# A hybrid encoder step on one core: the durations by which vector steps are woven between matrix products

## The chip, the cores and the metric

The kernel runs on one core of a Trainium2 chip. The metric is the device time of one execution in microseconds, the median of the runs shown. Its engines are named as in the profile: PE does matrix products, DVE elementwise vector work, ACT activations, POOL nearly nothing here, and SP issues the transfers.

## The reference

Two layers act on 1024 prompt rows and 32 sample rows of width 1024, with shared weights. Layer 0 mixes with a gated MLP, layer 1 with trailing means over windows of 2, 4, 8 and 16 rows. Each mixer is followed by a feed-forward of width 4096. Norms stand on both sides of each, and a conditioning vector gives shifts, scales and gates. Cut to its core:

```python
for i in range(DEPTH):                       # DEPTH = 2
    mod = jax.nn.silu(c) @ w_ada[i] + b_ada[i]
    sh1, sc1, gt1, sh2, sc2, gt2 = jnp.split(mod[:, None, :], N_MOD, axis=-1)
    h = rmsnorm(x, g_norm[i, 0]) * (1 + sc1) + sh1
    mix = sgu_mixer(h, ...) if i % 2 == 0 else pool_mixer(h_ext, ...)
    x = x + gt1 * rmsnorm(mix, g_norm[i, 1])
    h = rmsnorm(x, g_norm[i, 2]) * (1 + sc2) + sh2
    f = jnp.square(jax.nn.relu(h @ ffn_w_up[i])) @ ffn_w_down[i]
    x = x + gt2 * rmsnorm(f, g_norm[i, 3])
```

All of it is float32; the outputs are the two sequences and three small states.

## The kernel before

Columns are rows of the sequence: activations lie transposed, features on the partitions. There are three column tiles `t`: 384 and 384 prompt columns, and a last one of 256 prompt and 32 sample columns, so its elementwise work goes in two segments (`segs`). Per tile there is `acc[t]`, the running sum and later the residual stream, and `hh[t]` and `hl[t]`, the high and low parts of the normed input. Every product is three matrix products (`products`, L720 to L725): high weight by high input, high by low, low by high. A weight block is loaded to `raw`, copied to the high part `wh` on ACT (L342) and subtracted to the low part `wl` on DVE (L343).

**Order of the products.** The gating mixer works in groups `g` (`sgu_item`), the feed-forward in chunks `c` of 512 hidden features (`ffn_item`). Each item has an up part (`pu`, or `pf` in four blocks) and a down part (`po` or `pg`, eight blocks `d`), which adds into `acc[t]` on DVE (L875). The down part is held in `pending` and is written out in the middle of the next item. For layer 0 the last groups and chunks (6, 7) are done tile by tile, and for layer 1 the first chunks (0, 1) too, so that one tile's mixer or feed-forward can end, be normed and feed the next stage while the other tiles still have products. A down block whose item has an `after` ends a tile: it also squares each `acc` block for the norm (`Stat.square`).

**Fillers.** What happens to a tile between two stages is a generator, kept in `fillers`: `ffn0_t` (from gating mixer to feed-forward 0), `ffn1_t` (from feed-forward 0 through pooling mixer to feed-forward 1) and `out_t`. Its pieces are `Stat.finish` (the norm: two small products `pn` over the split sums `sc` and `sm`, L610 to L632), `residual` (gate and add the old stream, which is loaded again from memory, L644 to L672), `apply` (scale on DVE L689, shift on ACT L698, low part on DVE L699), the window sums (L1191 to L1219) and the mixing products `pp` (L1240). A generator yields after each step a number, the step's duration in us as the program counts it; a negative one says that the same filler goes on next. `weave(budget, streams)` is called after each block of products: it first does up to `streams` steps of the weight stream (1.1 each for a weight), then pulls filler steps until the budget is spent. Every third pull takes the second filler instead of the first. `finish(tag)` pulls until the named filler is through; it is called before the first chunk of a feed-forward needs that tile:

```python
while budget > 0 and fillers:
    budget -= pull()
...
if c == 0:
    finish(f"ffn{l}_{t}")
ffn_item(p, t, after if c == 7 else None)
```

The numbers set only the order in which instructions are written. The tile framework then places them on the engines; each engine works through its own queue in order and waits on semaphores. Sums sit in PSUM buffers: three for down parts (`pd`, which `pp` and early products share), two for up parts (`pu`), three for norms and transposes (`pm`).

Of the kernel before, what the change touches and what calls it, by code (L numbers as in the profile page):

```python
# [34 lines left out]
def tile_stream_encoder_step(  # L35
# [32 lines left out]
    def pool(name, **kw):  # L68
# [8 lines left out]
    ncol = [p + s for _, p, s in TILES]  # L77
    segs = [
        [(0, p, 0)] + ([(p, s, 1)] if s else []) for _, p, s in TILES
    ]  # L80
# [70 lines left out]
    for i, parts in enumerate(rows):  # L151
        n = sum(k for _, k in parts)
# [363 lines left out]
        wdone.add(key)  # L516


    fillers = deque()

    sticky = []
# [54 lines left out]
    class Stat:  # L576
# [42 lines left out]

        def finish(self, out):  # L620
            n = self.n
            yield 0.5
            pn = ps_ms(f"pn_{self.tag}")
            for i, x in enumerate(self.parts):
                mm(pn[:, :n], onesr, x[:, :n], start=i == 0, stop=i == 1)
            yield 0.3
            q = t_m(f"q_{self.tag}")[:, :n]
            r = work.tile([P, 384], F32, tag="rr", bufs=2, name=f"r_{self.tag}")[:, :n]
            act(out=r, in_=pn[:, :n], func=AF.Abs_reciprocal_sqrt, scale=1.0 / D)
            act(out=q, in_=r, func=AF.Square)  # L630
            stt(out=q, in0=pn[:, :n], scalar=-0.5 / D, in1=q, op0=ALU.mult, op1=ALU.mult)
            stt(out=r, in0=q, scalar=1.5, in1=r, op0=ALU.add, op1=ALU.mult)  # L632
            out.append(r)
            yield 2.0


    def residual(st, l, cf, tag, out, store=True, stat=True):
        t = st.t
        n = ncol[t]
        xos = {}  # L640

        def load(k2):
            xos[k2] = t_x(f"xo_{tag}_{k2}", [P, 2, n])
            nc.sync.dma_start(xos[k2], xd[t][:, 2 * k2 : 2 * k2 + 2, :])  # L644

        got = []
        yield from st.finish(got)
        r = got[0]
        st2 = Stat(t, tag + "x")
        for half in range(2):  # L650
            for k2 in (2 * half, 2 * half + 1):
                load(k2)
            for k2 in (2 * half, 2 * half + 1):
                for k in (2 * k2, 2 * k2 + 1):
                    for c0, w, v in segs[t]:
                        a = A(t, k, c0, w)
                        stt(
                            out=a,
                            in0=a,
                            scalar=coef[:, l, cf, v, k : k + 1],  # L660
                            in1=r[:, c0 : c0 + w],
                            op0=ALU.mult,
                            op1=ALU.mult,
                        )
                    yield -0.46
                a = acc[t][:, 2 * k2 : 2 * k2 + 2, HALO:]
                tt(out=a, in0=a, in1=xos[k2], op=ALU.add)
                if stat:
                    st2.square(2 * k2, a)
                yield 0.9 if k2 % 2 else -0.9  # L670
        if store:
            nc.sync.dma_start(xd[t], acc[t][:, :, HALO:])  # L672
        out.append(st2)
# [8 lines left out]
    def apply(t, l, cf, sh, r, keep=False):  # L682
        hh[t] = room("h", t, f"hh{l}_{cf}_{t}", F32R)
        hl[t] = room("l", t, f"hl{l}_{cf}_{t}", F32R)
        for k in range(KB):
            for c0, w, v in segs[t]:
                x = A(t, k, c0, w)
                a = t_m(f"mt{t}_{k}_{v}")[:, :w] if keep else x
                stt(  # L689
                    out=a,  # L690
                    in0=x,
                    scalar=coef[:, l, cf, v, k : k + 1],
                    in1=r[:, c0 : c0 + w],
                    op0=ALU.mult,
                    op1=ALU.mult,
                )
                b = mod[:, l, sh * 8 + k, v : v + 1]
                act(out=hh[t][:, k, c0 : c0 + w], in_=a, func=AF.Identity, bias=b, scale=1.0)  # L698
                stt(  # L699
                    out=hl[t][:, k, c0 : c0 + w],  # L700
                    in0=a,
                    scalar=b,
                    in1=hh[t][:, k, c0 : c0 + w].bitcast(F32),
                    op0=ALU.add,
                    op1=ALU.subtract,
                )
            yield 0.95

    def first_norm(t):
        n = ncol[t]  # L710
# [189 lines left out]
    def sgu_item(g, t, wt, bb, after):  # L900
        n = ncol[t]
# [65 lines left out]
        def down():  # L967
            for d in range(KB):
                ps = ps_dn(f"po{g}_{t}_{d}")
                wh, wl = need_w(("o", g, d // 4))  # L970
                terms = []
                for k in range(2):
                    o = k * 512 + (d % 4) * P
                    a, b = hid[k]
                    terms.append((wh[:, o : o + P], wl[:, o : o + P], a[:, :n], b[:, :n]))
                products(ps, n, terms)
                accumulate(t, d, ps, g == 0)
                if d == 0 and after is not None:
                    st = Stat(t, f"rs_{t}")
                if after is not None:  # L980
                    st.square(d)
                if t == NT - 1 and d % 4 == 3:
                    w_finish(("o", g, d // 4))
                weave(0.4, d % 2)
            if after is not None:
                after(st)

# [7 lines left out]
    def ffn_item(p, t, after):  # L995
        l, c, tiles = passes[p]
        last = t == tiles[-1]
        n = ncol[t]
        hid = []

        def up(j):
            ps = ps_up(f"pf{l}_{c}_{t}_{j}")
            products(ps, n, up_terms(("up", p, j), t))
            if last:
                w_finish(("up", p, j))
            r = t_m(f"r{l}_{c}_{t}_{j}")
            act(out=r[:, :n], in_=ps[:, :n], func=AF.Relu)  # L1007
            a, b = t_hid("h", f"fh{l}_{c}_{t}_{j}"), t_hid("l", f"fl{l}_{c}_{t}_{j}")
            act(out=r[:, :n], in_=r[:, :n], func=AF.Square)
            split(a, b, r, n)  # L1010
            hid.append((a, b))

        def down():
            for d in range(KB):
                ps = ps_dn(f"pg{l}_{c}_{t}_{d}")
                wh, wl = need_w(("dn", p, d // 2))
                terms = []
                for j in range(4):
                    o = j * 256 + (d % 2) * P
                    a, b = hid[j]  # L1020
                    terms.append((wh[:, o : o + P], wl[:, o : o + P], a[:, :n], b[:, :n]))
                products(ps, n, terms)
                accumulate(t, d, ps, c == 0)
                if d == 0 and after is not None:
                    st = Stat(t, f"rf{l}_{t}", l == 0 or t < NT - 1)
                if after is not None:
                    st.square(d)
                    if l == 1 and t == NT - 1:
                        scale_last(d)
                        if d > 0:  # L1030
                            turn_last(d - 1)
                if last and d % 2 == 1:
                    w_finish(("dn", p, d // 2))
                weave(1.3, d % 2)
            if after is not None:
                after(st)

        for j in range(4):
            up(j)
            weave(3.0)  # L1040
            if j == 0:
                flush()
        pending.append(down)


# [62 lines left out]
    def to_pool(st):  # L1108
        t = st.t
        n = ncol[t]  # L1110
        npr, nsm = TILES[t][1], TILES[t][2]

        def run():
# [25 lines left out]
            for k in range(KB):  # L1139
                for c0, w, v in segs[t]:  # L1140
                    a = A(t, k, c0, w)
                    stt(
                        out=a,
                        in0=a,
                        scalar=coef[:, 1, 0, v, k : k + 1],
                        in1=r[:, c0 : c0 + w],
                        op0=ALU.mult,
                        op1=ALU.mult,
                    )
                    dst = a if v == 0 else pool_ext["e"][:, k, 16 : 16 + w]  # L1150
                    act(
                        out=dst,
                        in_=a,
                        func=AF.Identity,
                        bias=mod[:, 1, k, v : v + 1],
                        scale=1.0,
                    )
                yield 0.5
            if t == 0:
                nc.vector.memset(acc[0][:, :, 0:HALO], 0.0)  # L1160
            if t + 1 < NT:
# [21 lines left out]
            for src, w, dst0, nm in parts:  # L1183
                for g in range(4):
# [3 lines left out]
                    for lev in range(g + 1):  # L1188
# [7 lines left out]
                        )  # L1196
                        cur = nxt
                        step *= 2
                        yield -0.9
                    body = cur[:, :, HALO:]  # L1200
                    hsrc = src[:, 2 * g : 2 * g + 2, HALO:]
                    dst = acc[t][:, 2 * g : 2 * g + 2, HALO + dst0 : HALO + dst0 + w]
# [21 lines left out]
                        op0=ALU.mult,  # L1224
                        op1=ALU.subtract,
                    )
                    yield 1.0 if g == 3 else -1.0

            sp = Stat(t, f"rp_{t}")
            for g in range(4):  # L1230
# [11 lines left out]
                for e in range(2):  # L1242
                    d = 2 * g + e
                    act(out=A(t, d), in_=pss[e][:, :n], func=AF.Copy, scale=pscale[:, d : d + 1])
                    sp.square(d)
                yield 0.3
            yield from mix_to_ffn(sp, 1)

        fillers.append((f"ffn1_{t}", run()))
# [124 lines left out]
```

## Time and profile before

| | us |
|---|---|
| runs before, median (lowest to highest) | 2258.66 (2256.62 to 2258.75) |
| profiled execution | 2254.32 |
| its span, first to last instruction | 2252.5 |
| mean granted clock of PE | 0.994 |
| PE busy | 2205.2 |
| DVE busy | 1308.7 |
| ACT busy | 867.9 |

The span is one execution of the program under the hardware profiler, and 1.8 us of that execution's own time lie outside it. Busy time is the sum of an engine's instructions. Each row of a wait names who waited, for whom, and the total, count and longest wait in us. A window row gives, for a stretch of the span, its length, each engine's busy time and instructions, the granted PE clock as a share of full speed, the share of the DMA engines, and GB/s. Stages by time: conditioning and value products to 293 us, gating groups to about 680, feed-forward 0 to about 1470, feed-forward 1 to the end.

### The profile page before, as it was taken

The page shows a single profiled execution, that of the slowest core. Times are in us where ns is not written, and L with a number is a line of the kernel's source. Part 1 is how long each engine was busy: PE and PEld are TensorE (multiplying, and loading weights), DVE is VectorE, ACT ScalarE, POOL GpSimd, SP SyncE. Part 2 cuts the span into 40 slices and gives each one's busy share as a digit, 9 for nine tenths or more (in the row PEclk, how much of TensorE's full clock was granted, in tenths as well). Part 3 has the DMA queues.
Part 4 walks back from the last instruction along what each step waited for, and adds up shares of the span by engine and source line. Part 5 has one row for each costly group of instructions (what it writes and reads, how often), then busy time and mean ns, then how long its engine had stood idle before and what let it go on. Part 6 is the DMA issues. An engine that isn't in the chain of part 4 may idle for free.

```text
span 2252.5 us, 33484 instructions
## 1 busy us (share of the span) xinstructions
PE 2205.2 (98%) x13508; PEld 2099.6 (93%) x13508; DVE 1308.7 (58%) x2677; ACT 867.9 (39%) x1579; POOL 0.7 (0%) x6
## 2 busy tenths in 40 slices
PE   7999999999999999999999999899999999999998
PEld 5777899999989999999999999789899999999998
DVE  4855756555698366584654579999752322323345
ACT  4633521112256413223232466676652322313334
POOL 0000000000000000000000000000000000000000
PEclk9999999999999999999999999999999999999999
DMA  8465532122143223233332454664550211202112
GB/s 295 149 225 163 179 98 84 60 72 67 53 133 106 94 85 113 85 120 95 95 103 71 134 157 148 195 181 153 190 169 10 66 38 38 75 10 66 41 50 91
DMA packets 269631, 245.34 MB, mean 109 GB/s; under 512 B 8642, under 2 KB 247690, under 8 KB 269476
## 3 DMA queue, kind: packets, MB, share of 16 engines
q1 hardware_dynamic: 269204, 243.10, 34.5%
q8 instruction: 106, 1.74, 0.3%
q14 instruction: 49, 0.40, 0.1%
q10 hardware_dynamic: 272, 0.10, 0.0%
HBM read 211.32 MB, written 31.84 MB: 108 GB/s over the span
## 4 chain that ended last, share of the span: by engine, by line
PE 90%; DVE 4%; ACT 2%; DMA 2%; issue 1%; SPq 0%; DVEq 0%; ACTq 0%
PE pf L723 11%; PE pf L724 11%; PE pf L725 11%; PE pg L723 10%; PE pg L724 10%; PE pg L725 10%; PE pu L723 3%; PE po L723 3%; PE pu L724 3%; PE pu L725 3%; PE po L724 3%; PE po L725 3%; PE pv L748 2%; PE pv L749 2%; PE pv L750 2%; PE psp L929 1%
## 5 line engine op out<-in xcount | busy, mean ns | idle before, releaser
L723 PE MATMUL pf<-hh,wh_up 128*128 128x384 f32 (+1 forms) x1536 | 499.8, 326 | 4.3 <-ACT hh L698 3.7
L724 PE MATMUL pf<-hl,wh_up 128*128 128x384 f32 (+1 forms) x1536 | 498.8, 325 | 1.2 <-DVE hl L699 1.2
L723 PE MATMUL pg<-fh,wh_dn 128*128 128x384 f32 (+1 forms) x1536 | 497.8, 325 | 1.0 <-DVE acc L875 0.9
L725 PE MATMUL pf<-hh,wl_up 128*128 128x384 f32 (+1 forms) x1536 | 497.1, 324 | 0.0
L724 PE MATMUL pg<-fl,wh_dn 128*128 128x384 f32 (+1 forms) x1536 | 495.4, 323 | 1.1 <-DVE fl L868 1.1
L725 PE MATMUL pg<-fh,wl_dn 128*128 128x384 f32 (+1 forms) x1536 | 494.8, 322 | 0.0
L875 DVE TENSOR_TENSOR acc<-acc,pg 128x384 f32<-128x384 f32 (+1 forms) x336 | 173.7, 519 | 271.2 <-PE pg L725 270.2
L723 PEld LDWEIGHTS pf<-hh,wh_up 128*128 128x128 f32 x1536 | 289.1, 188 | 9.0 <-ACT hh L698 4.2
L723 PEld LDWEIGHTS pg<-fh,wh_dn 128*128 128x128 f32 x1536 | 289.0, 188 | 4.6 <-issue 2.0
L724 PEld LDWEIGHTS pg<-fl,wh_dn 128*128 128x128 f32 x1536 | 289.1, 188 | 2.8 <-DVE fl L868 2.1
L724 PEld LDWEIGHTS pf<-hl,wh_up 128*128 128x128 f32 x1536 | 289.4, 188 | 2.1 <-DVE hl L699 1.5
L725 PEld LDWEIGHTS pf<-hh,wl_up 128*128 128x128 f32 x1536 | 289.3, 188 | 0.4
L725 PEld LDWEIGHTS pg<-fh,wl_dn 128*128 128x128 f32 x1536 | 288.9, 188 | 0.0
L414 DVE SCALAR_TENSOR_TENSOR aa<-raw,csil,aa 128x256 f32<-128x256 f32 x560 | 233.0, 479 | 3.2 <-DMA raw<-in_w_ada_dram 3.2
L1007 ACT ACTIVATE r<-pf 128x384 f32<-128x384 f32 (+1 forms) x192 | 87.5, 458 | 372.0 <-PE pf L725 357.1
L868 DVE TENSOR_TENSOR fl<-r,fh 128x384 fp32r<-128x384 f32 (+1 forms) x192 | 100.3, 522 | 179.9 <-ACT fh L867 165.6
L342 ACT ACTIVATE wh_up<-raw 128x1024 fp32r<-128x1024 f32 x96 | 101.6, 1058 | 262.7 <-PE pf L724 244.5
L343 DVE TENSOR_TENSOR wl_up<-raw,wh_up 128x1024 fp32r<-128x1024 f32 x96 | 117.5, 1224 | 122.2 <-ACT wh_up L342 122.0
L342 ACT ACTIVATE wh_dn<-raw 128x1024 fp32r<-128x1024 f32 x96 | 101.6, 1059 | 120.8 <-PE pg L724 107.2
L343 DVE TENSOR_TENSOR wl_dn<-raw,wh_dn 128x1024 fp32r<-128x1024 f32 x96 | 117.4, 1223 | 46.7 <-ACT wh_dn L342 46.6
L723 PE MATMUL po<-ush,wh_o 128*128 128x384 f32 (+1 forms) x384 | 127.5, 333 | 3.4 <-DVE acc L875 3.1
L723 PE MATMUL pu<-hh,wh_u 128*128 128x384 f32 (+1 forms) x384 | 126.6, 330 | 1.6 <-DVE s L945 1.6
(260 smaller groups left out, 2978.2 us busy)
## 6 DMA issues: line engine op xcount, KB each, us to landing
raw<-in_w_ada_dram SPq DMA_DIRECT2D x96, 512.0 KB, 3.9
raw<-in_ffn_w_up_dram SPq DMA_DIRECT2D x96, 512.0 KB, 4.1
raw<-in_ffn_w_down_dram SPq DMA_DIRECT2D x96, 512.0 KB, 3.4
raw<-in_sgu_w_in_dram SPq DMA_DIRECT2D x32, 512.0 KB, 4.6
xd<-acc SPq DMA_DIRECT2D x8, 1536.0 KB, 7.3
xo_r<-xd SPq DMA_DIRECT2D x32, 384.0 KB, 3.8
vd<-vt SPq DMA_DIRECT2D x32, 256.0 KB, 2.7
raw<-in_sgu_w_out_dram SPq DMA_DIRECT2D x16, 512.0 KB, 3.5
```

The lines of the kernel that those rows point to most:

```text
L342: act(out=wh, in_=r, func=AF.Copy)
L343: tt(out=wl, in0=r, in1=wh.bitcast(F32), op=ALU.subtract)
L414: stt(out=aa[:, v, :], in0=w, scalar=k, in1=aa[:, v, :], op0=ALU.mult, op1=ALU.add)
L723: mm(ps[:, :n], wh, rh, start=i == 0, stop=False)
L724: mm(ps[:, :n], wh, rl, start=False, stop=False)
L725: mm(ps[:, :n], wl, rh, start=False, stop=i == last)
L748: mm(ps[:m, :], a_h, wh[:, o : o + 512], start=k == 0, stop=False)
L749: mm(ps[:m, :], a_h, wl[:, o : o + 512], start=False, stop=False)
L750: mm(ps[:m, :], a_l, wh[:, o : o + 512], start=False, stop=k == KB - 1)
L868: tt(out=dst_lo[:, :n], in0=src[:, :n], in1=dst_hi[:, :n].bitcast(F32), op=ALU.subtract)
L875: tt(out=A(t, d), in0=A(t, d), in1=ps[:, :n], op=ALU.add)
L1007: act(out=r[:, :n], in_=ps[:, :n], func=AF.Relu)
```

## The change

A helper `dve(n, parts)` counts 0.15 us for each instruction and one 960th of a microsecond for each column. The fixed step numbers of norm, residual, modulation, windows and mixing are replaced by it. The residual's second step also counts the squares that it issues. In blocks that end a tile, the weave budget of the gating mixer's down block goes from 0.4 to 0.0, and that of the feed-forward's down block from 1.3 to 0.8.

For 384 columns `dve(n)` is 0.55, for two blocks of 384 columns 0.95, for 288 columns 0.45 and in two segments 0.60.

```diff
+    def dve(n, parts=1):
+        return 0.15 * parts + n / 960.0
...
         def finish(self, out):
             n = self.n
-            yield 0.5
+            yield dve(n)
             pn = ps_ms(f"pn_{self.tag}")
...
             out.append(r)
-            yield 2.0
+            yield 2 * dve(n)
...
     def residual(st, l, cf, tag, out, store=True, stat=True):
...
-                    yield -0.46
+                    yield -dve(n, len(segs[t]))
                 a = acc[t][:, 2 * k2 : 2 * k2 + 2, HALO:]
                 tt(out=a, in0=a, in1=xos[k2], op=ALU.add)
+                cost = dve(2 * n)
                 if stat:
                     st2.square(2 * k2, a)
-                yield 0.9 if k2 % 2 else -0.9
+                    cost += (k2 > 0) * dve(2 * n) + (k2 == 3) * 2 * dve(n)
+                yield cost if k2 % 2 else -cost
...
     def apply(t, l, cf, sh, r, keep=False):
...
-            yield 0.95
+            yield 2 * dve(ncol[t], len(segs[t]))
...
# sgu_item, down
-                weave(0.4, d % 2)
+                weave(0.4 if after is None else 0.0, d % 2)
...
# ffn_item, down
-                weave(1.3, d % 2)
+                weave(1.3 if after is None else 0.8, d % 2)
...
# to_pool: modulation, window levels, window ends, mixing
-                yield 0.5
+                yield dve(n, len(segs[t]))
...
-                        yield -0.9
+                        yield -dve(2 * w)
...
-                    yield 1.0 if g == 3 else -1.0
+                    yield dve(2 * w) if g == 3 else -dve(2 * w)
...
-                yield 0.3
+                yield 2 * dve(n)
             yield from mix_to_ffn(sp, 1)
```

## The prediction

> **What bounds the kernel now.** I read the page first, then PE's waits, then stage windows, then single rows.
>
> ```profile
> PE 2205.2 (98%) x13508; PEld 2099.6 (93%) x13508; DVE 1308.7 (58%) x2677; ACT 867.9 (39%) x1579; POOL 0.7 (0%) x6
> ```
>
> PE is busy 98% of the span and the change alters no product, so only PE's idle time and its clock can move. After 600 us PE idles 22 us: 8.5 at the first boundary (gating mixer to first feed-forward, 641 to 691), 10.8 at the second (pooling mixer, 1384 to 1482), 1.7 at the third (1593 to 1616), 1.3 in the tail. The waits at the first two, total, count, longest:
>
> ```profile
> PE pn_rs L625 <- ACT sc_rs L610: 3.6, 2, 2.2
> PE po L723 <- DVE acc L875: 2.8, 3, 1.3
> ...
> PE pf L723 <- ACT hh L698: 3.7, 1, 3.7
> PE pn_r_0x L625 <- ACT sc_r_0x L610: 2.1, 1, 2.1
> ```
>
> Each hangs on DVE's queue: `po` waits for an accumulation, `pn` for the squares' sum, `pf` for a modulated tile. The windows show DVE full there, and PE's clock halved behind the gaps:
>
> ```profile
> core 0: us, PE busy (x) PEld busy (x) DVE busy (x) ACT busy (x) POOL busy (x), PEclk, DMA share, GB/s
> 641.50:650.30 8.80, 3.65 (x13) 1.87 (x11) 8.80 (x17) 5.93 (x11) 0.00 (x0) 0.79 0.17 45
> ...
> 646.60:653.40 6.80, 4.47 (x16) 3.67 (x16) 6.39 (x15) 5.45 (x8) 0.00 (x0) 0.50 0.25 77
> ...
> 691.00:694.40 3.40, 3.40 (x11) 3.40 (x12) 3.40 (x7) 2.95 (x7) 0.00 (x0) 0.50 0.53 154
> ...
> 1393.00:1414.00 21.00, 21.00 (x150) 21.00 (x149) 20.47 (x33) 13.58 (x22) 0.00 (x0) 1.00 0.54 155
> 1414.00:1470.00 56.00, 46.53 (x292) 43.63 (x291) 51.21 (x85) 34.84 (x61) 0.00 (x0) 0.91 0.56 175
> ```
>
> So the local bound is DVE's order: what stands ahead of the instruction that PE needs next. Prices come from DVE's groups (mean ns last):
>
> ```profile
> L875 DVE TENSOR_TENSOR acc<-acc,po 128x384 f32<-128x384 f32 x18 | 9.8, 545 | 0.0
> L699 DVE SCALAR_TENSOR_TENSOR hl<-acc,mod,hh 128x384 fp32r<-128x384 f32 x16 | 9.5, 609 | 0.0
> L657 DVE SCALAR_TENSOR_TENSOR acc<-acc,coef,r_rs 128x384 f32<-128x384 f32 x16 | 9.5, 615 | 0.0
> L667 DVE TENSOR_TENSOR acc<-acc,xo_r 128x768 f32<-128x768 f32 x8 | 7.6, 953 | 0.0
> ```
>
> Successive rows overlap by 0.08 us, so a queue advances by the duration less 0.08: 0.46, 0.53, 0.53, 0.87; a weight split `wl` by 1.14. A product of 384 columns takes 0.173 us of PE (24 in 4.18), one of 288 columns 0.135 to 0.145.
>
> **What moves.** No instruction is added or removed; the same ones stand in another order on PE, DVE, ACT and SP. The new numbers make most steps dearer (a residual step with squares 0.9 to 1.9 or 3.0), one cheaper (the norm's end 2.0 to 1.1), the 32-column windows much cheaper (0.9 to 0.22). Dearer steps and smaller budgets push work towards the points where `finish` must pull all that is left. Stepping through the budgets, the steps pulled there go from 0 to 18 for `ffn0_0`, 0 to 22 for `ffn1_0`, 18 to 31 for `ffn1_1`, and from 25 down to 10 for `ffn1_2`. Since every third turn goes to the second filler and a step with a negative number keeps the turn, finishing tile 0 also drags in tile 1's residual.
>
> I summed DVE's new queue row by row with the traced durations, from the last instant that both orders share, and held it against PE's new queue.
>
> **A, first boundary, +0.6.** To 624.45 us nothing changes. Then tile 0's sixteen modulation instructions no longer stand among tile 1's accumulations and squares. DVE reaches tile 1's split `sm_rs` at 641.5 instead of 648.9; PE starts `pu` of group 7, tile 2 at 643.3 instead of 650.3, runs it at full clock, and is 7.9 ahead when `pf` of tile 0 begins (657.2 against 665.1). Meanwhile DVE has nothing to do from 644.5 to 647.6. From there 31.6 us of queue plus 1.1 of waits end with tile 0's last `hl` at 680.3; 11.3 of it is tile 1's residual (8 x 0.53, 4 x 0.87, 3 x 0.87, 1.0). PE loses 1.8 on tile 2's gate (`usl`) and has 5.7 us of products between 664.5 and 680.9, so idles 10.7. Given back: the wait for `pn_rs` of tile 2, 3.4 now, about 1.1 then (-2.3), and the half clock behind it (-1.7). Sum -7.9 + 1.8 + 10.7 - 2.3 - 1.7 = +0.6. Bounds: -2 if ACT never delays these chains, +5 if the accumulations of tile 2 fall behind too.
>
> **B, second boundary to the third `pf` of tile 0, 0.** The mixing products `pp` of tile 0 now come behind `pf` 1 and 2 of tile 2. DVE's queue between 1393 and 1414 then holds 8.9 us of work in place of 20.5, since the residual that filled it waits behind squares of `pp`. It resumes at 1414.2 and has 51.5 us, plus 1.7 of waits, up to tile 0's last `hl`: 1467.4, against 1453.2. PE, 3.4 ahead at first, waits 5.4 for `sm_r_0x` (1442 to 1447.4), 3.8 for the accumulation that frees a `pd` buffer, runs some 3 us at half clock, and is through the two `pf` blocks at 1468.5 to 1470.1. Before it was there at 1469.5, having idled 9.9. Bounds -1 and +3.5.
>
> **C, second boundary to the last `pf` of tile 1, +10.5.** DVE starves again while PE does `pp` of tile 1 (8 us idle between 1500 and 1512), for the window steps that filled this are already done; tile 1's last `hl` comes at 1557.4 instead of 1546.8. On PE: 3.4 by 1516.7 (1513.3 before), from `pd` buffers and the squares' sum; then 2.0 for `sm_r_1x`, 4.5 for the accumulation of `pg` 0, now behind the residual in DVE's queue, and 0.9 for tile 2's statistics, less 0.3. Sum +10.5: `pf` 3 of tile 1 starts at 1569.5 instead of 1559.0. Bounds +3.4 (the three waits find cover) and +16 (ACT, whose queue I summed only where a row waits for it, adds its latency, up to 2.85 us in the trace from the last product of a `pf` to its `fl`: 1363.2 to 1366.06).
>
> **D, third boundary, -0.2.** The 1.7 us of idle goes, because `ffn1_2` is nearly done when it is called for; 1.5 comes, for `pp` of tile 2 waiting on the last window. DVE had 12 us idle between 1579 and 1604, which absorbs its lag. Bounds -1.7 and +2.
>
> **E, clock, +1.7.** The trace halves the clock for 3.4 us after gaps of 2.16 us (ending 688.9) and 2.07 us (ending 1417.3), for 6.8 after longer ones. C's new 6.5 us gap gets one 3.4 us window, 1.7 lost; 0 if a wait hides it, 3.4 for two. The Trainium skill, TensorE: Matmul & The Clock Gate, "What's actually happening", asks for at least one idle window of about 3.4 us before the half rate; by that rule the 2 us gaps would have been free, which the trace contradicts, and E would still be 1.7, its gap being longer.
>
> **F, tail and transfers, 0.** Tile 1's 24 output transposes move about two `pg` blocks later, among the products that end at 2242 us; PE does them all the same, +-0.5. On SP the residual loads move with their steps past weight loads. Their three shared buffers come free 4 to 20 us ahead of use in the new queue (a load lands in 4.6), so nothing; a load that lands late would cost those 4.6.
>
> Sum: 0.6 + 0 + 10.5 - 0.2 + 1.7 = 12.6. On the profiled execution's 2254.3 (span 2252.5 and 1.8 around it) this gives 2266.9; the median shown is 4.3 above that execution, so I state 2271.
>
> **Rivals.**
> 1. *The stalls go and nothing replaces them* (faster). Place: 641.5 to 653.4 and 1415 to 1459. Returned: 7.9 at the first, 2.3 and 1.7 behind it, 4 at the second (the 2.07 wait and its clock): some -13 at most, -10 likely, 2248.7. For it: DVE's 8.8 of 8.8 us full while PE does 3.65, just where the budgets shrink. It decides if tile 0's last `hl` comes before PE has used its products, 664.5 + 5.7 = 670 at the first boundary; my sum has 680.3, so DVE would have to be 10 us quicker than its traced rows.
> 2. *A zero-sum shift* (no change): DVE is full through both boundaries whatever the order, and C's delay is caught up in DVE's later slack; A, B, D only, 2258.7 to 2260. For it: A and B come out even. Against: DVE's new idle (3 + 12 + 8 us) is time that a full engine loses.
> 3. *The numbers don't take hold*: PE's order is set later, by the layer that places instructions. The first products of `pf` and `po` interleave there in both orders, but PE's new queue differs from the old in 169 places, all at these boundaries and in the tail; 2258.7.
>
> **Chances.** Forecast 0.64, +5 to +25 by the bounds taken together in part, 2264 to 2284. Rival 1 0.21; rivals 2 and 3 0.15 together. A measurement of this kernel can tell about 0.2%, 4.5 us. Rival 2 sends a little to either side: faster 0.21, same 0.14, slower 0.65. For 8 in 10 the range leaves out the lower half of rival 1 and the top of the forecast: 2250 to 2284.
>
> **What would show it.** Right: the 641 to 650 waits on `acc` and `sc_rs` gone, a new PE wait on `hh`/`hl` (L698, L699 of before) of about 10 us near 665 to 681, DVE busy under half of 1395 to 1414, and PE waits on `sm_r`/`acc` of 5 us or more near 1445 and 1540. Wrong: PE idle after 600 us below 20, or the wait on `hh` near 665 under 4 us; then the queue ahead of tile 0 was shorter than I summed.

## The result and the profile after

| | before | after |
|---|---|---|
| median of the runs, us (lowest to highest) | 2258.7 (2256.6 to 2262.5) | 2279.3 (2277.8 to 2281.1) |
| span of the profiled execution | 2252.5 | 2277.6 |
| mean granted PE clock | 0.994 | 0.985 |

The ratio is 1.0099 [1.0087, 1.0111], 22 us; the medians of the table are 20.6 us apart. So the change makes the kernel slower. The forecast was slower, 2271 in 2250 to 2284. The page's totals after:

```profile
PE 2216.1 (97%) x13508; PEld 2108.8 (93%) x13508; DVE 1309.1 (57%) x2677; ACT 870.9 (38%) x1579; POOL 0.7 (0%) x6
```

DVE does the same work in the same time. PE is busy 10.9 us longer with the same products, because more of them run at half clock, and the rest of the 25.1 us of span is PE idling. DVE's groups of the changed kernel have the old prices (lines after L516 stand 4 to 6 lower in the file):

```profile
L671 DVE TENSOR_TENSOR acc<-acc,xo_r 128x768 f32<-128x768 f32 x32 | 30.4, 951 | 0.0
L705 DVE SCALAR_TENSOR_TENSOR hl<-acc,mod,hh 128x384 fp32r<-128x384 f32 x32 | 19.1, 611 | 0.0
```

PE's waits after (total, count, longest):

```profile
PE pg L729 <- DVE acc L881: 9.5, 5, 4.3
PE pf L729 <- ACT hh L704: 7.4, 5, 4.3
PE pn_r_0x L629 <- ACT sc_r_0x L614: 5.0, 1, 5.0
...
PE pf L731 <- DVE wl_up L343: 1.8, 1, 1.8
```

The waits for `pn_rs` and `po` that stood high in the list before have gone from the top. `pg` on accumulations has taken their place, and two have grown: `pf` on modulated tiles from 3.7 to 7.4, `pn_r_0x` from 2.1 to 5.0. Stage windows after:

```profile
core 0: us, PE busy (x) PEld busy (x) DVE busy (x) ACT busy (x) POOL busy (x), PEclk, DMA share, GB/s
641.50:650.30 8.80, 8.14 (x58) 7.47 (x57) 5.36 (x13) 6.11 (x9) 0.00 (x0) 1.00 0.37 104
671.80:685.45 13.65, 9.16 (x26) 7.25 (x25) 13.09 (x22) 6.06 (x9) 0.00 (x0) 0.50 0.56 185
1395.00:1414.00 19.00, 18.31 (x92) 13.85 (x92) 9.37 (x15) 15.08 (x29) 0.00 (x0) 1.00 0.55 171
1446.60:1460.25 13.65, 7.32 (x27) 6.51 (x28) 12.52 (x20) 6.75 (x11) 0.00 (x0) 0.50 0.77 263
1484.20:1494.40 10.20, 7.14 (x21) 6.55 (x22) 10.20 (x15) 6.22 (x11) 0.00 (x0) 0.50 0.69 202
1500.00:1520.00 20.00, 20.00 (x90) 15.76 (x89) 11.60 (x15) 14.18 (x26) 0.00 (x0) 1.00 0.60 190
1549.00:1562.65 13.65, 10.00 (x34) 8.95 (x35) 12.93 (x26) 7.01 (x12) 0.00 (x0) 0.50 0.52 166
```

Two things are to be seen. The first stall is gone: PE does 8.1 of 8.8 us of work where it did 3.7. And DVE, full before at 1393 to 1414, is idle half the time there and again at 1500 to 1520, where the kernel before had it nearly full:

```profile
1495.00:1515.00 20.00, 19.98 (x115) 19.64 (x114) 19.20 (x34) 15.05 (x26) 0.00 (x0) 1.00 0.76 235
```

Each later gap on PE is followed by 10 to 14 us at half clock. DVE's own waits say what it idles for, first in 1395 to 1414, then in 1500 to 1520:

```profile
DVE sq_rp L602 <- ACT sq_rp L593: 5.5, 6, 1.4
DVE wl_up L343 <- ACT wh_up L342: 4.0, 3, 2.0
```

```profile
DVE sq_rp L602 <- ACT sq_rp L593: 7.5, 6, 3.0
```

The rows of `sq_rp` are squares of the mixing products `pp`, so DVE runs at the pace of the `pp` blocks; the row of `wl_up` is weight splits that wait for the copy on ACT. DVE has 15 instructions in the first stretch, where the kernel before had 33 in 21 us.

**The same by stages.** A stage's edges are the first product of a named block, so that kernels can be compared whatever lies ahead of it. A: `po` 3 of group 7, tile 1 (632.6 before) to `pf` 3 of chunk 0, tile 1. B: chunk 7's first product to `pf` 2 of tile 0, layer 1. C: from there to `pf` 3 of tile 1. D: to `pf` 3 of tile 2. "Clock" is half of PE's busy time in stretches at half clock.

| | A | B | C | D |
|---|---|---|---|---|
| before: length, idle, clock | 92.6, 8.7, 4.0 | 203.4, 9.9, 3.9 | 89.5, 1.0, 0 | 78.9, 1.8, 0 |
| after: length, idle, clock | 94.5, 9.8, 4.6 | 204.1, 11.4, 3.7 | 108.5, 11.2, 8.6 | 80.1, 3.0, 0 |
| difference of length | +1.9 | +0.7 | +19.0 | +1.2 |
| forecast (E's 1.7 was laid to C) | +0.6 | 0 | +10.5 and 1.7 | -0.2 |

The profiled execution after comes to A 3.0 us later. It has this lag already at DVE's last row ahead of the first that the change moved (616.1 for 613.1), and keeps it to A; part of it is a stretch of 3.4 us at half clock at 255 us. The executions of the kernels below lie between 632.6 and 637.5 at this point, so this is no effect of the change. Of the 25.1 us of span 22.8 come in A to D, nearly all of it in C.

### The profile page after: what moved, and what is told of

Its sections match the earlier page's. It is cut to its first block, busy times and chain, and to the rows that moved or that the text cites. A ratio compares the mean times of both kernels' runs of the same rounds, so it can differ in the third digit from the quotient of the medians.

```text
span 2277.6 us, 33508 instructions
## 1 busy us (share of the span) xinstructions
PE 2216.1 (97%) x13508; PEld 2108.8 (93%) x13508; DVE 1309.1 (57%) x2677; ACT 870.9 (38%) x1579; POOL 0.7 (0%) x6
## 4 chain that ended last, share of the span: by engine, by line
PE 89%; DVE 5%; DMA 3%; ACT 2%; issue 1%; SPq 0%; DVEq 0%; ACTq 0%
PE pg L729 10%; PE pf L729 10%; PE pf L730 10%; PE pg L731 10%; PE pf L731 10%; PE pg L730 10%; PE pu L729 3%; PE po L729 3%; PE pu L730 3%; PE pu L731 3%; PE po L730 2%; PE po L731 2%; PE pv L754 2%; PE pv L755 2%; PE pv L756 2%; PE psp L935 1%
## 5 line engine op out<-in xcount | busy, mean ns | idle before, releaser
L729 PEld LDWEIGHTS pg<-fh,wh_dn 128*128 128x128 f32 x1536 | 291.0, 189 | 15.2 <-DVE acc L881 10.5
```

Of the source, the lines that this page charges most:

```text
L729: mm(ps[:, :n], wh, rh, start=i == 0, stop=False)
```

## The experiments

The theory after the first result, T1: what counts is how late a tile's chain of vector work stands in DVE's queue. Dearer steps and smaller budgets leave it to `finish`; DVE first starves, then has everything at once, and PE waits. Rivals: the budgets alone or the durations alone do it; the half clock does it by itself. "Above before" is the ratio to the kernel before, run beside each, times its median of 2257. All stage differences are to before, and each is of one profiled execution. Three kernels below have the same order in A (durations only, gating budget back, first boundary only) and give -1.8, -3.4 and -2.0 there, so a difference under 2 us in one stage says little by itself.

**Only the budgets.** The kernel before with 0.0 and 0.8.

```diff
-                weave(0.4, d % 2)
+                weave(0.4 if after is None else 0.0, d % 2)
...
-                weave(1.3, d % 2)
+                weave(1.3 if after is None else 0.8, d % 2)
```

> Only the two smaller budgets (0.0 and 0.8 in blocks that end a tile), with the old durations. Pulled inside finish: 16 steps for ffn0_0 (before 0, changed kernel 18), 2 for ffn1_0 (0, 22), 31 for ffn1_1 (18, 31), 21 for ffn1_2 (25, 10). Theory 1 (cost goes with what finish has to pull, tile by tile): the first boundary behaves as in the changed kernel, +1 to +3 us there; tile 0 of the second boundary stays as before; tile 1 loses part of what the changed kernel loses, +4 to +10; 2264 to 2272 in all. Theory 2 (the durations alone shift the order, the budgets only decide where a step is written): within 4 us of 2258.7. Theory 3 (the budgets are the whole of it): 2275 or more.

Measured 2260.7, ratio 1.0018 [1.0009, 1.0028], 4.1 us above before. Stages: A +0.3, B -0.8, C +4.9, D -0.9. Below the 2264 of T1, but C's part is as T1 had it.

**Only the durations.** The changed kernel with 0.4 and 1.3.

> Only the new durations, with the old budgets (0.4 and 1.3). Pulled inside finish: 0 for ffn0_0, 14 for ffn0_1, 9 for ffn1_0, 28 for ffn1_1, 10 for ffn1_2. Theory 1 (cost goes with what finish has to pull): the first boundary as before or a little better (the 641 to 650 us waits stay), the second loses 8 to 14 us of the changed kernel's 19.7; 2266 to 2273. Theory 2 (the durations are the whole of it): 2275 or more. Theory 3 (budgets are the whole of it): within 4 us of 2258.7.

Measured 2264.6, ratio 1.0034 [1.0020, 1.0047], 7.7 above, a little under T1's 2266, with C's loss as T1 had it. A -1.8, B -4.1, C +13.7, D +1.0. The halves cost 4.1 and 7.7, together 22: they add up to half of it. Neither alone is the cause, and C is where both of them pay.

**The named filler only.**

```diff
         while any(f[0] == tag for f in fillers):
+            turn[0] = 2
             pull()
```

> The changed kernel, but finish pulls the named filler only, without every third turn for the second. Pulled inside finish: ffn0_0 5 (18 before this edit, 13 of them tile 1's), ffn1_0 14 (22, 11 of them tile 1's), ffn1_1 24 (31, 14 of them tile 2's), ffn1_2 24 (10), ffn0_1 11 (4). Theory 1 (tile 1's residual ahead of tile 0 in DVE's queue is what PE waits for): the 4.27 us wait on hh at 675 and the 3.08 us wait at 1451 go, with half clock behind them; 8 to 15 us faster than the changed kernel, 2264 to 2271. Theory 2 (DVE has to do the same work before PE can go on, whichever tile comes first; the stall moves to tile 1 and 2): within 3 us of 2279. Theory 3: the third boundary, with 24 steps in finish instead of 10, loses what the first two gain, also within 3 us, but with idle time at 1580 to 1640 of 5 us or more.

Measured 2270.4, ratio 1.0059 [1.0044, 1.0074], 13.3 above, so 9 us better than the changed kernel. A -1.0 (and +0.6 behind it), B -0.9, C +15.9, D -0.7. The waits on `hh` in A, 4.3 the longest, are gone, and one of 1.7 on the relu's `r` stands there. But tile 1's residual is only put off: a wait of 4.4 for `pn_r_2x` follows at about 720. The turn for the second filler costs 2 to 3 us in each stage; C stays, with one wait of 8.9 for an accumulation.

**Larger budgets, new durations.**

```diff
-                weave(0.4, d % 2)
+                weave(0.6, d % 2)
...
-                weave(1.3, d % 2)
+                weave(2.0, d % 2)
```

> The new durations with larger budgets: 0.6 for each down block of the gating mixer (0.4 before) and 2.0 for each of the feed-forward (1.3 before), ending or not. Pulled inside finish: 0 for ffn0_0, ffn0_1 and ffn1_0, 8 for ffn1_1, 1 for ffn1_2 (the durations alone: 0, 14, 9, 28, 10). The durations alone gave +5.9 us at the stages up to pf 2 of tile 0, but -13.7 in the stage of tile 1. Theory 1 (what finish has to pull sets the loss, so a budget that leaves nothing to pull takes it away): the stage of tile 1 loses 0 to 5 us instead of 13.7, the total comes to the time of before or up to 6 us below. Theory 2 (DVE is full at the boundaries, more steps between products only move the wait to the accumulations, as at 641 to 650 us before): waits on acc grow, the total is 3 to 12 us above before.

Measured 2271.9, ratio 1.0066 [1.0049, 1.0083], 14.9 above. C is -2.2, with 0.1 us of idle: with 8 steps left for `finish` there, in place of 28 with the durations alone, the stage's whole loss has gone. But A is +1.9, B +7.0 and D +5.9. PE's waits now:

```profile
PE pn_r_1x L629 <- ACT sc_r_1x L614: 7.6, 1, 7.6
PE pn_rs L629 <- ACT sc_rs L614: 6.7, 2, 5.6
```

The total is above what either theory gave, but each shows in a stage: work left over is paid at `finish`, work pulled early is paid at the sums that wait behind it. The budget moves the loss between the stages.

**Single durations set back, from the changed kernel.** First the mixing step, then the residual's second step:

```diff
-                yield 2 * dve(n)
+                yield 0.3
             yield from mix_to_ffn(sp, 1)
```

> The changed kernel, with the step of the mixing products back at 0.3 (1.1 in the changed kernel). Pulled inside finish: 18, 4, 18, 28, 10 (the changed kernel 18, 4, 22, 31, 10). Theory 1 (DVE starves at 1393 to 1414 and 1500 to 1512 us because the mixing products come too late): DVE is over half busy in these stretches again and 5 to 10 us of the 22 come back. Theory 2 (the number of steps left for finish decides, and it hardly changes): within 3 us of the changed kernel, 20 to 22 us above before.

```diff
-                yield cost if k2 % 2 else -cost
+                yield 0.9 if k2 % 2 else -0.9
```

> The changed kernel, with the residual's second step back at 0.9 for all (0.95, 1.9 and 3.0 in the changed kernel, for the squares that it issues). Pulled inside finish: 18, 4, 20, 31, 9 (the changed kernel 18, 4, 22, 31, 10). Theory 1 (the number of steps left for finish decides): within 3 us of the changed kernel. Theory 2 (the residual's larger numbers are what spreads the work and make the loss): 8 us or more of the 22 come back.

Measured 2279.0, ratio 1.0097 [1.0082, 1.0112], C +17.7; and 2276.5, ratio 1.0085 [1.0070, 1.0100], C +18.4. Neither alone returns anything that counts; DVE stays starved, with 7.5 and 9.4 us of work in the 19 us that were 1395 to 1414 in the changed kernel.

**Both set back, with the old budgets.** The durations-only kernel with both edits.

> The new durations with the old budgets, but the two that grew most set back: the residual's second step at 0.9 (0.95, 1.9, 3.0 in the change) and the mixing step at 0.3 (1.1). What stays changed: the norm's end 2.0 to 1.1, the modulation 0.95 to 1.1, the first residual step 0.46 to 0.55, the windows 0.9 to 0.95 and, of 32 columns, to 0.22. Pulled inside finish: 14 for ffn0_1, 5 for ffn1_0, 24 for ffn1_1, 8 for ffn1_2 (all durations: 14, 9, 28, 10). Theory 1 (those two numbers make the stage of tile 1 longer by 13.7 us): it comes to within 5 us of before, and the total to 2254 to 2260. Theory 2 (the loss hangs on many small numbers and on whose turn it is, not on these two): the stage keeps 9 us or more of the 13.7, the total 6 to 10 us above before.

Measured 2255.5, ratio 0.9996 [0.9986, 1.0006]. A -1.2, B -6.3, C +4.6, D +1.8. As the first theory here had it, these two numbers together make 9 of the 13.7 us in C; one of them alone with the old budgets was not run. The stretches that starved are full again:

```profile
1395.00:1414.00 19.00, 19.00 (x133) 18.64 (x133) 18.27 (x30) 14.78 (x27) 0.00 (x0) 1.00 0.51 152
1500.00:1520.00 20.00, 20.00 (x116) 20.00 (x116) 19.93 (x33) 14.01 (x22) 0.00 (x0) 1.00 0.70 213
```

**The gating budget back.** The changed kernel with 0.4 for the gating mixer alone.

> The changed kernel, with the gating mixer's budget back at 0.4 in blocks that end a tile; the feed-forward's stays 0.8. Pulled inside finish: 0, 14, 22, 31, 10 (the changed kernel 18, 4, 22, 31, 10; the durations alone 0, 14, 9, 28, 10). Theory 1 (each boundary pays for its own budget): the first boundary as with the durations alone, 1.8 us shorter than before instead of 1.9 longer; the second as in the changed kernel; 16 to 20 us above before. Theory 2 (the turns of the two fillers, shifted at the first boundary, decide the second too): the stage of tile 1 differs from the changed kernel's by 4 us or more.

Measured 2270.8, ratio 1.0067 [1.0053, 1.0081], 15.1 above, just under the 16 expected. A -3.4, B -0.6, C +18.0, D +1.4: the first boundary pays for its own budget, 5.3 us, and the second does not notice.

**DVE's idle time over all of these.** From `pf` 0 of chunk 7, tile 1, through C:

| | length against before | DVE idle against before (13.2) |
|---|---|---|
| changed kernel | +19.7 | +18.1 |
| mixing step back | +18.8 | +18.0 |
| gating budget back | +17.4 | +15.7 |
| residual step back | +16.3 | +14.7 |
| named filler only | +15.0 | +14.7 |
| durations only | +9.6 | +8.4 |
| larger budgets | +4.7 | +0.6 |
| budgets only | +4.1 | +3.1 |
| both steps back, old budgets | -1.8 | -1.5 |

What the stretch gains in length is what DVE idles in it, within 2 us but for the larger budgets. That follows from DVE's having the same work in it each time (212.6 to 216.7 us busy), and ACT's idle time grows alike, from 75.8 to 92.9 in the changed kernel. So the table says how much is lost, not which engine causes it. That DVE bounds the stretch rests on PE's waits, which end at its rows or behind them, and on the kernel with both steps back. DVE is busy 58% of the span, but 94% of this stretch before (212.6 of 225.8), and PE 95%.

**Is it the clock? Filling the gaps.** In the changed kernel PE idles 1.6, 0.7 and 4.3 us from 1545 on, and 13.65 us of half clock follow, 5.0 us by the products in it. The edit adds products without use, in unused columns of sums that are at hand, so that PE is not idle; PE's order is else the same but for a few small products behind them. First 41 of the kernel's fast float32 form:

```diff
                 products(ps, n, terms)
+                for _ in range(FILL_DN.get((l, c, t, d), 0)):
+                    mm(ps[:, n:512], onesr, hid[3][0][:, : 512 - n], start=True, stop=True)
...
             for i, x in enumerate(self.parts):
                 mm(pn[:, :n], onesr, x[:, :n], start=i == 0, stop=i == 1)
+            for _ in range(FILL_PN.get(self.tag, 0)):
+                mm(pn[:, 384:512], onesr, self.parts[1][:, :P], start=True, stop=True)
```

> The changed kernel with 41 added matrix products of 128 columns (13 into unused columns of pg block 2 of chunk 1, tile 0; 28 into unused columns of the norm's sum of tile 1) that fill PE's idle time at 1545 to 1553 us; their results are not used. It asks what the half clock behind that gap costs by itself: 13.65 us at half clock with 10.0 us of work, 5.0 us lost. Theory 1 (the clock loss is real time, term E was mis-sized): the 13.65 us stretch shrinks to 3.4 us or nothing, 3 to 5 us faster than the changed kernel, 2274 to 2276. Theory 2 (what follows waits for DVE anyway, so full clock only turns into idle): within 1.5 us of 2279. Theory 3 (the added products delay the norm): slower than 2280.

```profile
1545.10:1548.51 3.41, 2.47 (x19) 2.19 (x19) 3.41 (x9) 0.94 (x2) 0.00 (x0) 1.00 1.01 368
1548.51:1558.75 10.24, 9.90 (x41) 9.06 (x40) 8.56 (x18) 4.29 (x8) 0.00 (x0) 0.50 0.70 221
```

Measured 2278.9, ratio 1.0094 [1.0078, 1.0111]. The question was not answered: with PE 2.47 of 3.41 us busy the clock fell all the same, and the second set then took 5.4 us for 28 products. Next, 25 in plain float32:

```diff
+                    mm(ps[:, n:512], ones, hid[3][0][:, : 512 - n].bitcast(F32), start=True, stop=True)
...
+                mm(pn[:, 384:512], ones, self.parts[1][:, :P].bitcast(F32), start=True, stop=True)
```

> The changed kernel with 25 added products in plain float32 of 128 columns (8 and 17 in the two gaps at 1545 to 1553 us, their results not used). The earlier fill of 41 products of the fast float32 form left PE busy in the records, and the clock still fell to half for 10.2 us. A plain float32 product of 128 columns takes 0.218 us of PE in the profile (two rows of 0.109 apart) where the fast form's took 0.125, with the same columns. Theory 1 (the gate goes by the work of the array, not by whether a product stands in the records, and the half clock costs real time): no half clock at 1549 to 1563, 3 to 5 us faster than the changed kernel. Theory 2 (the half clock follows the wait, not the array's idleness, so that it comes anyway): 10 to 14 us at half clock there as before, within 1.5 us of the changed kernel. Theory 3 (the clock stays full but the next products wait for DVE anyway): no half clock, within 1.5 us all the same.

```profile
1545.28:1548.69 3.41, 2.74 (x22) 2.44 (x22) 3.41 (x9) 1.19 (x2) 0.00 (x0) 1.00 0.93 339
1548.69:1552.10 3.41, 3.02 (x28) 2.82 (x26) 3.41 (x7) 2.10 (x4) 0.00 (x0) 1.00 0.13 46
1582.83:1589.65 6.82, 2.14 (x9) 1.82 (x8) 6.82 (x11) 1.61 (x4) 0.00 (x0) 0.75 0.30 84
```

Measured 2276.8 (2273.5 to 2279.4), ratio 1.0086 [1.0071, 1.0102]; the interval overlaps that of the changed kernel. Now the clock stays full, and C is 4.5 us shorter than after. D is 4.7 longer: a new gap at 1582 to 1588, with half clock of its own. PE waits there for a weight split:

```profile
PE pf L735 <- DVE wl_up L345: 4.7, 1, 4.7
```

and DVE's timeline (start, duration, instruction, idle before it) shows what stands ahead of the split:

```profile
1579.99 1.36 DVE L1203 TENSOR_TENSOR win2p<-acc 128x542 f32<-128x542 f32 x2 [2.09 <-DMA out_dram<-stp_p]
...
1583.57 0.72 DVE L1203 TENSOR_TENSOR win2p<-acc 128x542 f32<-128x542 f32 x1
...
1586.89 1.22 DVE L345 TENSOR_TENSOR wl_up<-raw,wh_up 128x1024 fp32r<-128x1024 f32 x1
```

Tile 2's window sums, which wait for the store of the pooling state to free a buffer. DVE's chain has hardly moved: tile 1's last `hl` ends 1.2 us earlier than in the changed kernel, tile 2's 0.4 (each counted from the start of A). PE, 5.2 us ahead at `pf` 3 of tile 1, meets the split sooner and is 2.3 ahead behind it; the new half clock, 2.5 us by the products in it, takes the rest. So in this execution the time won in C is lost in D, half by waiting and half by the clock.

**The same fill in the kernel before,** ahead of the two waits of 2 us, five plain float32 products each.

```diff
                 products(ps, n, terms)
+                if (g, t, d) == (7, 2, 7):
+                    for _ in range(5):
+                        mm(ps[:, n:512], ones, hid[1][0][:, : 512 - n].bitcast(F32), start=True, stop=True)
...
             products(ps, n, up_terms(("up", p, j), t))
+            if (l, c, t, j) == (0, 7, 2, 0):
+                for _ in range(5):
+                    mm(ps[:, n:512], ones, hh[t][:, 0, : 512 - n].bitcast(F32), start=True, stop=True)
```

> The kernel before, with 10 added plain float32 products of 224 columns (5 in unused columns behind the last down block of the gating mixer, 5 behind pf block 0 of chunk 7, tile 2; their results not used), ahead of the two waits of 2.16 and 2.07 us behind which the clock is halved for 3.4 us while PE is 3.41 of 3.41 us busy. PE's order is otherwise that of before. One takes about 0.38 us (0.218 for 128 columns in the profile), five 1.9. Theory 1 (half clock costs real time where PE has products to do): the two stretches at 691 and 1418 us go, 1.7 us each, 2 to 3.5 us below before. Theory 2 (PE's lead is lost again at the next wait for DVE): the stretches go, and the time is within 1 us of before. Theory 3 (the added products delay what PE owes DVE): slower.

Measured 2257.9, ratio 1.0005 [0.9996, 1.0014]: nothing gained. The stretch at 1418 is gone, but the next one, behind the wait on `hh`, is 10.2 us instead of 6.8; the one at 691 stayed. Tile 0's last `hl` ends at 1453.1, counted from the start of A, in the kernel before at 1453.2.

**A version that beats both.** The kernel before, with the new durations for norm, residual and modulation of the first boundary only (tags `rs`, `r1_0`, and `apply` with `(l, cf) == (0, 2)`):

```diff
...
-                    yield -0.46
+                    yield -dve(n, len(segs[t])) if tag[:4] == "r1_0" else -0.46
...
+                if tag[:4] == "r1_0":
+                    cost = dve(2 * n) + (k2 > 0) * dve(2 * n) + (k2 == 3) * 2 * dve(n)
+                yield cost if k2 % 2 else -cost
...
-            yield 0.95
+            yield 2 * dve(ncol[t], len(segs[t])) if (l, cf) == (0, 2) else 0.95
```

> The kernel before, with the new durations for the first boundary alone (norm, residual and modulation from gating mixer to feed-forward 0); all other numbers and both budgets as before. Pulled inside finish: ffn0_1 14 (before 3), the rest as before. Theory 1 (stages pay on their own): the first boundary 1.8 us shorter, as in the run of the durations alone, nothing else moves; 0 to 3 us below before. Theory 2 (that gain came from the other numbers, or is eaten later): within 1 us of before, or above.

Measured 2254.1, ratio 0.9987 [0.9978, 0.9996], 2.9 us below before. A -2.0, the other stages within 0.5. The wait for `pn_rs` of tile 2 that stood at 687 is replaced by a shorter one for `pn_r_1x` (1.2 for 2.2).

## Why the prediction was right in sign and short in size

The sum was 12.6, the ratio says 22.4, the medians 20.6. Most of the signs that it named came: the waits at 641 to 650 are gone, DVE is busy under half of 1395 to 1414, and PE waits 5.0 on the statistics of tile 0's new residual. The wait on `hh`, named as about 10, came to 6.5 in pieces, and the longest near 1540 is 4.3, not 5. Times below are counted on the clock of the kernel before, from the start of A.

- **A held,** within its bounds. Tile 0's last `hl` was summed to 680.3 and came at 680.8. PE's wait ahead of these blocks was summed as 10.7 in one piece; it came as 0.8 for `s`, and 2.0 and 4.3 for `hh`, since PE's products between them ran at half clock. +1.9 in bounds of -2 to +5.
- **B held** on PE (+0.7), though tile 0's last `hl` came at 1470.5, not 1467.4.
- **C, with the clock in it, is what was mis-sized:** +10.5 and E's 1.7 summed, +19.0 measured, above C's bound of +16. Its idle time came as summed: +10.2, with `pg` waiting 4.3 (4.5 summed) and `pn_r_1x` 2.3 (2.0). That agreement is in part luck: two errors stand against each other in it, PE slower by the clock than summed (E below) and DVE later. DVE's queue was summed too short: tile 1's last `hl` at 1557.4, measured 1565.0, 7.6 late. The starving was there as summed (9.6 us idle in 1395 to 1414, 8.4 in 1500 to 1520). Missing were DVE's small waits after the starving, most of them for ACT: 1.7 us were allowed, up to tile 0's last `hl` only. The windows of the changed kernel have 5.0 in 1414 to 1475, 2.2 in 1475 to 1500 and 2.1 in 1520 to 1565, 9.3 in all:

```profile
1414.00:1475.00 61.00, 50.34 (x323) 47.39 (x321) 56.00 (x93) 35.15 (x59) 0.00 (x0) 0.89 0.53 166
1475.00:1500.00 25.00, 20.32 (x95) 18.84 (x96) 22.84 (x35) 15.17 (x28) 0.00 (x0) 0.80 0.46 135
1520.00:1565.00 45.00, 38.42 (x192) 36.09 (x192) 42.86 (x80) 27.40 (x46) 0.00 (x0) 0.85 0.55 176
```

  The upper bound, +16, named ACT's latency as the risk and still priced it once, not per wait.
- **D:** +1.2 against -0.2. What is new on PE is a wait of 1.85 us for a split of `wl_up`, which stands behind tile 2's windows in DVE's queue; the windows, not the weights, are late.
- **E was mis-sized.** One stretch of 3.4 us was allowed, up to 3.4 us lost. C alone has 23.9 us at half clock, 8.6 lost, so on PE's side the 7 us that C's sum lacks are all clock; on DVE's side they are the late `hl`. How much of them each causes is open. The second fill made C 4.5 us shorter with tile 1's last `hl` only 1.2 earlier, so within C the clock had a price of its own; that time was lost again in D. Two of its four executions lie near 2274, with a mean clock of 0.991, and two near 2279, with 0.988; the profiled one is of the latter. So half clock may well cost this kernel some 5 us where no new gap follows; the ratio does not tell it from nothing. In the kernel before, the fill took away one stretch at half clock and gained nothing.
- **F:** nothing moved in the tail: from D's end to the last product 604.5 before, 603.8 after.
- **The rivals:** the zero-sum shift holds for A and B and fails in C; the numbers took hold. The first rival, that the stalls go and nothing takes their place, was right that the wait at 641 to 650 goes. Its terms, 7.9, 2.3, 1.7 and 4, add to 15.9, not to 13. The last kernel above has some of what it priced behind the first stall, with the new order at the first boundary and the budget of 0.4; the stall itself stays there (PE does 4.4 of the 8.9 us). That the stage's own trade decides was not in the sum: at the old budgets the new durations make A and B shorter by 5.9.

## What to carry to other kernels

An engine busy 57% of the span can be nearly full in the stage that counts: sum its queue over the stage, with every wait on the engines that feed it, and expect time that it idles there to be missing later. A weaving budget does not remove vector work, it chooses whether the tile that ends or the tile that follows pays, so it is tuned per boundary, and a duration that is truer on average can be the worse number at one place. Clock lost behind a gap is not a price of its own until filling the gap has shown that the next instruction was ready.

## What the runs showed of the hardware

Over the 14 profiled executions here, from 20 us on and up to the last product, the clock changes only on a fixed grid of 3.41 us, and the choice goes with how much PE idled in the window before, in several small gaps or in one. Of 60 windows at full clock with 1.85 us or more of idle, all were followed by half clock; of 196 with 0.25 to 1.25 us, one was; of the 47 between, 18. Back to full it takes more: of 73 windows at half clock with more than 0.51 us idle none was followed by full clock, of 84 with less than 0.2 us all but 5 were. Behind the gaps of 1.6, 0.7 and 4.3 us in the changed kernel it stayed down for four windows, 13.65 us, of which only the first was idle. The Trainium skill, TensorE: Matmul & The Clock Gate, "What's actually happening", has a free-running window of 3413 ns, which the grid bears out, and half rate after at least one idle window, which it does not: 54% of a window is enough.

The one exception among the 196 is the window of the first fill, with 0.94 us idle. Its added products of the fast form, of 128 columns, follow each other by 0.11 us, where those of 384 columns do by 0.173. So PE stood as busy in the records for longer per column, and in this one window the record of busy time was not the measure that the clock went by.
